# Moving a small projection from the first MLP to the end of layer 0's mixer, with one shared ring of scratch tiles

## The chip, the cores and the metric

The kernel runs on one core of a Trainium2 chip. The metric is the time of one execution on the device in microseconds (us), as the median of several runs; beside them stands one execution that was recorded by the hardware profiler, with a time of its own. Engines are named as the profile names them: PE is TensorE's matmuls and PEld its weight loads, DVE is VectorE, ACT is ScalarE, POOL is GpSimd, SP is SyncE, which here only issues the transfers of the weights.

## The reference, cut to what matters

A trunk of two layers works on x, 512 positions by 1024 features. Layer 0 mixes with a pair of recurrences (HGRN2 and RWKV-7), layer 1 with block attention. Each layer then has an MLP, and at its end a second input `p` (512 by 256 per layer) is projected, normalized and added through a gate:

```python
    for l in range(DEPTH):
        h = rms_norm(x, attn_norm[l])
        ...
        x = x + mix.astype(x.dtype)
        h = rms_norm(x, mlp_norm[l])
        x = x + jnp.square(jax.nn.relu(h @ w_up[l])) @ w_down[l]
        ple = rms_norm(p[l] @ ple_proj[l], ple_norm[l])
        x = x + ple * jax.nn.sigmoid(x @ ple_gate[l])
    return x
```

The line with `ple` depends on `p` and weights alone, not on x. It may be computed at any time before the gate of its layer.

## The kernel before, in words

**Tiles and products.** x lies transposed in SBUF as eight tiles of 128 features by 512 positions. Every large product is a `gemm` (line 240): a weight tile is stationary, 512 positions move, and each product is made of three matmuls, because weights and activations are split into a high and a low part (`mm3`, line 235). `wnext` (line 214) brings the weights: SyncE loads a half piece of 128 by 512 (line 223), ScalarE casts it to the high part `whi` (line 228), VectorE subtracts to get the low part `wlo` (line 229). The pieces come in a fixed order. While the mixer of layer 0 runs, there is one set of rings, two raw tiles and three of each part (`wa`, line 987). From the first MLP on a second set of three and four joins it (`wb`, line 992), so seven of each part.

**The order of the work.** The program is written as one long trace, and a planner turns it into a fixed order of instructions on each engine: it takes the instruction that was traced earliest among those whose inputs and buffers are ready by its estimate. So the text's order is a priority: what stands later fills gaps. `tc.high_priority` (line 720) puts the chain of the RWKV heads ahead of the rest. The work around the change comes in this order (`ORDER`, line 32, for four heads h):

- For each head: RWKV pieces (`step`, line 900, letters A and C), projections and HGRN recurrence (F, H), projections of the next head (B), and the output projection of the head before (O: `out_piece`, line 865). `hgrn` (line 731) takes its scratch from a ring of six tiles, `Hh` (line 364, `HB` in line 27), and its PSUM from `pmh`, a ring of two. Results of a head are split into tiles named `os`.
- `out_piece(3)` (line 928) stands alone behind the last head. Its eight evacuations add into x, then split and scale the new x for the MLP (`post`, line 979; lines 272 and 273) and square it (line 305), and GpSimd adds the squares up (`NormAcc`, line 311).
- The first MLP (`mlp`, line 1008). Its first four output tiles stay in PSUM (`pmr`, four tiles) until the row scale of the norm has been computed (`later_norm`, line 942): a chain of some ten tiny VectorE instructions on 128 by 4 values (lines 253 to 262, 292), then a broadcast over TensorE (`bcast_rows`, line 318, L326 in the profile).

**Delayed work.** `later` (line 933) holds functions with a count. `flush` (line 935) is called at each evacuation of the MLP's up projection and of the output projection, lowers each count and calls those that have run out. A count of 0 means the first call, 1 the second, and so on.

**The projection of the second input** is `ple` (line 949). It loads two tiles of `p` on ScalarE's queue (line 954), splits them into `act2` in layer 0 and `act` in layer 1, and multiplies two pieces of weights, each two half pieces giving four output tiles of 6 matmuls, through `pmh` (line 963): 48 matmuls. Each output tile is copied by ScalarE (line 959), squared by it, and GpSimd adds the squares. `finish` (line 966) computes the row scale, halves it (line 968), broadcasts it, and multiplies the eight tiles on VectorE (line 971). In layer 0 the projection itself is delayed (`PD` = 1, line 31): it is traced at the second evacuation of the first MLP, and `finish` four evacuations behind it (`FD` = 3, line 29). In layer 1 the projection is traced ahead of the attention's output projection (lines 1213 and 1214), and `finish` at the fourth evacuation of that. The eight output tiles are a pool of their own, `plp` (lines 1206 and 1212), until the gate (`gate`, line 1044) has read them.

**The values of the attention**, `vt` (line 1174), are one tile of 4 by 1024 per partition, written by ScalarE in eight pieces of 512 (line 1190) and read in slices of 128 columns (line 1167).

Of the kernel before, what the change touches and what calls it, by code (L numbers as in the profile page):

```python
# [11 lines left out]
F32 = mybir.dt.float32  # L12
F32R = mybir.dt.float32r
# [164 lines left out]
def trunk(ctx, tc, wts, xT, pT, vecs, lora, cst, lev, seg, rope, out, upto="all", dbg=None, mode=None):  # L178
# [97 lines left out]
    class Stats:  # L276
        def __init__(self, pool, tag, cols=1):
            self.n, self.cols, self.i = 1, cols, 0
            self.ps = pool.tile([P, 512], F32, name=tag)
# [16 lines left out]
            return (y, m) if both else y  # L296

    class NormAcc:
        def __init__(self, ring):
            self.ring, self.t = ring, None  # L300

        def add(self, src, eng="act"):
            sq = nrm.tile([P, S], F32, name="acc") if self.t is None else self.ring()
            if eng == "act":
                A.activation(sq, src, AF.Square)  # L305
            else:
                V.tensor_mul(sq, src, src)
            if self.t is None:
                self.t = sq
            else:  # L310
                G.tensor_add(self.t, self.t, sq)  # L311
# [39 lines left out]
    def chain(*gens):  # L351
        for g_ in gens:
            yield from g_


    def layer0_mixer(actp):
        ph = ExitStack()
# [3 lines left out]
        def E(name="e", bufs=EB, shape=None, dt=F32):  # L361
            return ex.tile(shape or [P, S], dt, name=name, bufs=bufs)

        def Hh():
            return ex.tile([P, S], F32, name="h", bufs=HB)

        BH = mp.tile([P, 2, 4, P], F32, name="BH")
        NAs = [mp.tile([P, 2, 2, 2, P], F32, name=f"NA{i}") for i in range(2)]
# [509 lines left out]

        lbo = VEC["lb"][0]
        e = [vec[:, lbo + 4 * i:lbo + 4 * i + 4] for i in range(3)]  # L880
        mx = mp.tile([P, 4], F32, name="lbm")
        V.tensor_max(mx, e[0], e[1])
        V.tensor_max(mx, mx, e[2])
        ee = mp.tile([P, 3, 4], F32, name="lbe")
        for i in range(3):
            V.tensor_sub(ee[:, i, :], e[i], mx)
        A.activation(ee, ee, AF.Exp)
        den = mp.tile([P, 4], F32, name="lbd")
        V.tensor_add(den, ee[:, 0, :], ee[:, 1, :])
        V.tensor_add(den, den, ee[:, 2, :])  # L890
        V.reciprocal(den, den)
        lb = mp.tile([P, 4], F32, name="lb")
        V.tensor_mul(lb, ee[:, 0, :], den)
        c1 = mp.tile([P, 4], F32, name="c1")
        V.tensor_scalar(c1, lb, 0.5, 0.5, op0=OP.mult, op1=OP.add)
        c2 = mp.tile([P, 4], F32, name="c2")
        V.tensor_scalar(c2, lb, -0.5, 0.5, op0=OP.mult, op1=OP.add)

        run(pre_h(0), p1(0, 0))
# [25 lines left out]
        for h in range(4):  # L925
            for c in ORDER:
                step(c, h)
        out_piece(3)
        ph.close()
        return acc, xg  # L930


    later = []

    def flush():
        for e in later[:]:
# [9 lines left out]
        later.append([n, lambda: nf.append(norm_rows(rt[0])[1])])  # L946
        return nf

    def ple(l, plp):
        pl = [plp.tile([P, S], F32, name=f"ple{m}") for m in range(8)]  # L950
        ps_ = []
        for k in range(2):
            t = tmp.tile([P, S], F32, name="r")
            nc.scalar.dma_start(t, pT[l, :, k, :])
            ps_.append(split(act if l else act2, t, "act" if l else "act2"))
        st = NormAcc(lambda: tmp.tile([P, S], F32, name="xsq"))

        def evac(m, ps):
            A.copy(pl[m], ps)
            st.add(pl[m])  # L960
        def body():
            for c in range(2):
                gemm(wnext(f"ple{l}", c), ps_, lambda m, ps: evac(4 * c + m, ps), nk=2, ring=pmh)
            later.append([FD[l], finish])

        def finish():
            rt = st.rs("n")
            V.tensor_scalar(rt, rt, 0.5, None, op0=OP.mult)
            rb = bcast_rows(rt, 1, pmh, "pmh")
            for m in range(8):  # L970
                V.scalar_tensor_tensor(pl[m], pl[m], vcol(f"pn{l}", m), rb, op0=OP.mult, op1=OP.mult)
        if l:
            body()
        else:
            later.append([PD, body])
        return pl

    act = ctx.enter_context(tc.tile_pool(name="act", bufs=16))
    def post(m, st, pool, tag, scale, dst):
# [6 lines left out]

    wa = wpool("wa", 2, 3)
    W["sets"] = [wa]
    st, xg = layer0_mixer(act)
    if upto == "mix0":  # L990
        return
    wb = wpool("wb", WB[0], WB[1])
# [71 lines left out]
    def attention(st, xg):  # L1064
# [72 lines left out]
        def head(h):  # L1137
            q, k, rq, nq = t.pop(h)
            pts = []
            for i in range(NJ):  # L1140
                n = (i + 1) * P
                ps = pmr.tile([P, S], F32, name="pmr")
                T.matmul(ps[:, :n], q[:, i * P:n], k[:, :n], start=True, stop=False)  # L1143
                T.matmul(ps[:, i * P:n], idb, cb, start=False, stop=True)
                mx = small.tile([P, 1], F32, name="mx")
                V.reduce_max(mx, ps[:, :n], axis=AX.X)
                V.tensor_mul(mx, mx, nq[:, i:i + 1])
                pt = ax.tile([P, n], F32, name=f"pt{i}")
                sm = small.tile([P, 1], F32, name="sm")
                A.activation(pt, ps[:, :n], AF.Exp, bias=mx, scale=rq[:, i:i + 1], accum_out=sm)  # L1150
                V.reciprocal(sm, sm)
                SCALE(pt, sm)
                pts.append(pt)
                yield
            pv = []
            for j in range(NJ):
                n = (NJ - j) * P
                ps = pmr.tile([P, S], F32, name="pmr")
                for i in range(j, NJ):
                    T.transpose(ps[:, (i - j) * P:(i - j + 1) * P], pts[i][:, j * P:j * P + P], ident)  # L1160
                tp = ax.tile([P, n], F32, name=f"pv{j}")
                A.copy(tp, ps[:, :n])
                pv.append(tp)
                yield
            ps = pmr.tile([P, S], F32, name="pmr")
            for j in range(NJ):
                T.matmul(ps[:, j * P:], vt[:, j, h * P:h * P + P], pv[j], start=j == 0, stop=j == NJ - 1)  # L1167
            res[h] = split(act2, ps, "act2")
            yield

        def SCALE(pt, sm):
            V.tensor_scalar(pt, pt, sm, None, op0=OP.mult)

        vt = ap.tile([P, NJ, D], F32, name="vt")

        def values(g, pools, after=None):
            ps = [p_.tile([P, S], F32, name=RING[p_]) for p_ in pools]
            for i in range(4):
                for z, (wh, wl) in enumerate(wnext("qkv", 4 * g + i)):
                    k = 2 * i + z  # L1180
                    for j in range(NJ):
                        xh, xl = (c[:, j * P:j * P + P] for c in xg[k])
                        T.matmul(ps[j], xh, wh, start=k == 0, stop=False)
                        T.matmul(ps[j], xh, wl, start=False, stop=False)
                        T.matmul(ps[j], xl, wh, start=False, stop=k == 7)
                if i == 1 and g == 0:
                    t["n"], m = st.rs("n", True)
                    V.tensor_scalar(e2, m, P * EPS, None, op0=OP.mult)
            for j in range(NJ):
                A.activation(vt[:, j, g * S:g * S + S], ps[j], AF.Copy, scale=t["n"][:, j:j + 1])  # L1190

        tc.keep_in_program_order(nc.scalar.preload_act_table_set("natural_log_exp_and_others"))
        values(0, [pmr] * 4)
# [9 lines left out]
        ph.close()  # L1203
        return [res[h] for h in range(8)]

    with tc.tile_pool(name="plp", bufs=1) as plp:
        nf = later_norm(st, ND[0])
        pl = ple(0, plp)
        xs = mlp(0, nf, xg)
        st, xg = gate(0, xs, pl)  # L1210
    o = attention(st, xg)
    with tc.tile_pool(name="plp", bufs=1) as plp:
        pl = ple(1, plp)
        st, xg = proj_out("o", o, 1)
        xs = mlp(1, later_norm(st, ND[1]), xg)
        gate(1, xs, pl)


OUT_SHAPE = (P, 8, S)
# [29 lines left out]
```

## Time and profile before

| | us |
|---|---|
| median of 3 runs (lowest to highest) | 1527.61 (1524.42 to 1528.14) |
| the profiled execution, its own time | 1525.94 |
| its span, from the first to the last instruction | 1524.2 |
| PE busy | 1487.4 (98%) |
| PEld busy | 1205.2 (79%) |
| DVE busy | 937.8 (62%) |
| ACT busy | 651.1 (43%) |
| POOL busy | 154.7 (10%) |

The mean granted clock of TensorE over the span is 0.997 of full. The span is about 1.7 us shorter than the execution's own time; that is the time around it. Times in the rows below count from the start of the span. Layer 0's mixer runs to about 465, the first MLP to about 820, its gate and the attention to about 1084, the attention's output projection to about 1128, and the second MLP and gate to the end.

A busy time of PE includes the pipeline: successive matmuls overlap, so the step from one start to the next is the time that one takes of the engine, and the length of one is longer. "[1.98 <-ACT os L269]" behind an instruction says that its engine had nothing to do for 1.98 us and that ScalarE's line 269, writing `os`, ended the wait.

### The profile page before, as it was taken

To read this page: it belongs to the slowest core of one execution; us is meant where nothing else is said; L and a number is where in the kernel's file an instruction comes from. 1 tells how busy PE (TensorE), PEld (TensorE's weight loads), DVE (VectorE), ACT (ScalarE), POOL (GpSimd) and SP (SyncE) were. 2 spreads that over 40 slices of the span, in tenths; PEclk is the share of its full clock that TensorE was granted. 3 is DMA by queue.
4 is the path that set the end of the run, shared out by engine and by line. 5 is a ranking of instruction groups with operands and counts; after the bars stand their busy time and mean duration, and the time that the engine had idled before them with its cause. 6 is when DMAs were issued, how large, how long until landed. Compare 5 with 4: busy or idle time off the path is not lost.

```text
span 1524.2 us, 20743 instructions
## 1 busy us (share of the span) xinstructions
PE 1487.4 (98%) x7656; PEld 1205.2 (79%) x7656; DVE 937.8 (62%) x1854; ACT 651.1 (43%) x1269; POOL 154.7 (10%) x145
## 2 busy tenths in 40 slices
PE   7999999999989999999999999999999999999998
PEld 5687787777667888888888888777778888888887
DVE  6877697686776644444446737777565444444463
ACT  3574544554446333333334533445634333333332
POOL 5221231211214000000000200000310000000000
PEclk9999999999999999999999999999999999999999
DMA  4211111201123333333333432111223333333331
GB/s 155 78 43 29 41 43 40 70 29 47 38 69 120 95 97 97 97 97 97 97 97 97 124 111 79 56 56 42 77 83 97 97 97 97 97 97 97 97 97 69
DMA packets 66966, 123.64 MB, mean 81 GB/s; under 512 B 7616, under 2 KB 8000, under 8 KB 66864
## 3 DMA queue, kind: packets, MB, share of 16 engines
q1 hardware_dynamic: 65376, 118.57, 25.6%
q10 hardware_dynamic: 1008, 2.16, 0.5%
q0 software_dynamic: 480, 1.57, 0.3%
q8 instruction: 60, 0.98, 0.3%
q14 instruction: 42, 0.34, 0.1%
HBM read 120.18 MB, written 2.10 MB: 80 GB/s over the span
## 4 chain that ended last, share of the span: by engine, by line
PE 90%; DVE 5%; ACT 2%; issue 1%; POOL 1%; DMA 1%; SPq 0%; DVEq 0%; POOLq 0%; ACTq 0%
PE pj L236 22%; PE pj L238 22%; PE pj L237 22%; PE pmr L237 2%; PE pmr L238 2%; PE pmr L236 2%; PE pmh L283 1%; PE pmr L1143 1%; PE pmr L1167 1%; PE pmr L596 1%; PE pmh L784 1%; DVE wlo L229 1%; DVE act L273 1%; PE pmr L532 1%; PE pmr L1160 1%
## 5 line engine op out<-in xcount | busy, mean ns | idle before, releaser
L228 ACT CAST whi<-wr 128x512 fp32r<-128x512 f32 x436 | 270.1, 621 | 605.2 <-PE pj L237 490.5
L229 DVE TENSOR_TENSOR wlo<-wr,whi 128x512 fp32r<-128x512 f32 x436 | 318.4, 733 | 215.5 <-ACT whi L228 195.9
L236 PE MATMUL pj<-act,whi 128*128 128x512 f32 (+1 forms) x968 | 384.3, 397 | 0.9 <-DVE h L858 0.9
L237 PE MATMUL pj<-act,whi 128*128 128x512 f32 (+1 forms) x968 | 381.9, 395 | 0.0
L238 PE MATMUL pj<-act,wlo 128*128 128x512 f32 (+1 forms) x968 | 381.4, 394 | 0.5 <-DVE wlo L229 0.5
L236 PEld LDWEIGHTS pj<-act,whi 128*128 128x128 f32 x968 | 182.6, 189 | 38.9 <-issue 2.3
L238 PEld LDWEIGHTS pj<-act,wlo 128*128 128x128 f32 x968 | 182.5, 189 | 36.9 <-DVE wlo L229 1.2
L237 PEld LDWEIGHTS pj<-act,whi 128*128 128x128 f32 x968 | 182.7, 189 | 35.0 <-issue 1.2
L238 PE MATMUL pj<-hid,wlo 128*128 128x512 f32 x512 | 199.4, 389 | 0.0
L237 PE MATMUL pj<-hid,whi 128*128 128x512 f32 x512 | 199.3, 389 | 0.0
L236 PE MATMUL pj<-hid,whi 128*128 128x512 f32 x512 | 199.3, 389 | 0.0
L1033 DVE TENSOR_TENSOR x<-x,pj 128x512 f32<-128x512 f32 x128 | 88.0, 688 | 80.7 <-PE pj L238 80.2
L236 PEld LDWEIGHTS pj<-hid,whi 128*128 128x128 f32 x512 | 96.1, 188 | 20.0
L238 PEld LDWEIGHTS pj<-hid,wlo 128*128 128x128 f32 x512 | 96.1, 188 | 20.0
L237 PEld LDWEIGHTS pj<-hid,whi 128*128 128x128 f32 x512 | 96.1, 188 | 19.9
L311 POOL TENSOR_TENSOR acc<-acc,xsq 128x512 f32<-128x512 f32 x28 | 38.6, 1379 | 627.3 <-ACT xsq L305 602.4
L1022 DVE SCALAR_TENSOR_TENSOR r<-pj,rb 128x512 f32<-128x512 f32 x56 | 38.7, 691 | 86.7 <-PE pj L238 86.7
L270 DVE TENSOR_TENSOR hid<-r,hid 128x512 fp32r<-128x512 f32 x64 | 44.3, 692 | 43.2 <-ACT hid L269 43.0
L236 PE MATMUL pmr<-act,whi 128*128 128x512 f32 x112 | 45.7, 412 | 6.7 <-ACT whi L228 6.7
L237 PE MATMUL pmr<-act,whi 128*128 128x512 f32 x112 | 45.7, 411 | 4.4 <-DVE act L273 4.4
L1023 ACT ACTIVATE r<-r 128x512 f32<-128x512 f32 x64 | 40.4, 632 | 20.9 <-DVE r L1022 20.9
L238 PE MATMUL pmr<-act,wlo 128*128 128x512 f32 x112 | 44.9, 405 | 0.0
(410 smaller groups left out, 2009.0 us busy)
## 6 DMA issues: line engine op xcount, KB each, us to landing
wr<-in_wts_dram SPq DMA_DIRECT2D x436, 256.0 KB, 2.7
x<-in_xT_dram SPq DMA_DIRECT2D x8, 256.0 KB, 6.5
out_dram<-x SPq DMA_DIRECT2D x7, 256.0 KB, 2.0
r<-in_pT_dram ACTq DMA_DIRECT2D x4, 256.0 KB, 3.7
lw<-in_lora_dram POOLq DMA_DIRECT2D x4, 192.0 KB, 3.1
tqn<-in_rope_dram ACTq DMA_DIRECT2D x1, 512.0 KB, 5.7
tkn<-in_rope_dram ACTq DMA_DIRECT2D x1, 512.0 KB, 6.2
cs<-in_cst_dram POOLq DMA_DIRECT2D x1, 289.0 KB, 5.8
```

What stands on the lines that cost most here:

```text
L228: A.copy(hi, raw)
L229: V.tensor_sub(lo, raw, hi.bitcast(F32))
L236: T.matmul(ps, wh, xh, start=first, stop=False)
L237: T.matmul(ps, wh, xl, start=False, stop=False)
L238: T.matmul(ps, wl, xh, start=False, stop=last)
L270: V.tensor_sub(l, src, h.bitcast(F32))
L273: V.scalar_tensor_tensor(l, src, scale, h.bitcast(F32), op0=OP.mult, op1=OP.subtract)
L283: T.matmul(self.ps[:, j * self.cols:(j + 1) * self.cols], sq[:, j * P:(j + 1) * P], rhs, start=(self.i == 0 and j == 0), stop=(self.i == s ...
L311: G.tensor_add(self.t, self.t, sq)
L1022: V.scalar_tensor_tensor(r, q, 0.0, nf[0], op0=OP.max, op1=OP.mult)
L1023: A.activation(r, r, AF.Square)
L1033: V.tensor_add(x[k], x[k], ps)
```

## The change

- In layer 0 the projection of the second input is traced at the end of the mixer, behind the last head's steps and ahead of `out_piece(3)`. It takes its working tiles from rings of the mixer that the last head no longer needs (`bo` and `y` for the loaded input, `r`, `k`, `v` and `kh` for its parts, `u` for the sum of squares, `e` for squares), and the weights through the mixer's one set of rings.
- `finish` is cut in two: `rows` computes and halves the row scale, `finish` broadcasts it and multiplies. In layer 0 `rows` is traced right behind `out_piece(3)` and `finish` at the second evacuation of the MLP. In layer 1 `rows` comes at the fourth evacuation of the output projection, where all of `finish` came before, and `finish` at the sixth.
- One ring `hp` of eight tiles named `h` takes the place of the mixer's ring of six, of the pool `plp`, and of `vt`: the mixer's scratch, the projection's eight results of each layer, and the eight tiles of the values take their turns in it.
- Four small tiles of the mixer are merged into two.

```diff
     class NormAcc:
-        def __init__(self, ring):
+        def __init__(self, ring, first=None):
             self.ring, self.t = ring, None
+            self.first = first or (lambda: nrm.tile([P, S], F32, name="acc"))
 
         def add(self, src, eng="act"):
-            sq = nrm.tile([P, S], F32, name="acc") if self.t is None else self.ring()
+            sq = self.first() if self.t is None else self.ring()
...
+    later = []
+    hp = None
+
+    def wide():
+        return hp.tile([P, S], F32, name="h")
+
...
-        def Hh():
-            return ex.tile([P, S], F32, name="h", bufs=HB)
+        Hh = wide
...
-        mx = mp.tile([P, 4], F32, name="lbm")
+        lbs = mp.tile([P, 2, 4], F32, name="lbs")
+        mx, den = lbs[:, 0, :], lbs[:, 1, :]
...
-        den = mp.tile([P, 4], F32, name="lbd")
...
-        c1 = mp.tile([P, 4], F32, name="c1")
+        cc12 = mp.tile([P, 2, 4], F32, name="c12")
+        c1, c2 = cc12[:, 0, :], cc12[:, 1, :]
         V.tensor_scalar(c1, lb, 0.5, 0.5, op0=OP.mult, op1=OP.add)
-        c2 = mp.tile([P, 4], F32, name="c2")
...
             for c in ORDER:
                 step(c, h)
+        pl, rows, finish = ple(0, lambda k: E("y" if k else "bo", 2),
+                               lambda i: E("r k v kh".split()[i], 1, dt=F32R),
+                               NormAcc(E, lambda: E("u", 1)))
         out_piece(3)
+        rows()
+        later.append([PD, finish])
         ph.close()
-        return acc, xg
-
-
-    later = []
+        return acc, xg, pl
+
...
-    def ple(l, plp):
-        pl = [plp.tile([P, S], F32, name=f"ple{m}") for m in range(8)]
+    def ple(l, raw, parts, st):
+
         ps_ = []
         for k in range(2):
-            t = tmp.tile([P, S], F32, name="r")
+            t = raw(k)
             nc.scalar.dma_start(t, pT[l, :, k, :])
-            ps_.append(split(act if l else act2, t, "act" if l else "act2"))
-        st = NormAcc(lambda: tmp.tile([P, S], F32, name="xsq"))
+            h, lo_ = parts(2 * k), parts(2 * k + 1)
+            A.copy(h, t)
+            V.tensor_sub(lo_, t, h.bitcast(F32))
+            ps_.append((h, lo_))
+        pl = []
 
         def evac(m, ps):
-            A.copy(pl[m], ps)
-            st.add(pl[m])
-        def body():
-            for c in range(2):
-                gemm(wnext(f"ple{l}", c), ps_, lambda m, ps: evac(4 * c + m, ps), nk=2, ring=pmh)
-            later.append([FD[l], finish])
+            t = wide()
+            A.copy(t, ps)
+            st.add(t)
+            pl.append(t)
+        for c in range(2):
+            gemm(wnext(f"ple{l}", c), ps_, evac, nk=2, ring=pmh)
+        rt = []
+
+        def rows():
+            r = st.rs("n")
+            V.tensor_scalar(r, r, 0.5, None, op0=OP.mult)
+            rt.append(r)
 
         def finish():
-            rt = st.rs("n")
-            V.tensor_scalar(rt, rt, 0.5, None, op0=OP.mult)
-            rb = bcast_rows(rt, 1, pmh, "pmh")
+            rb = bcast_rows(rt[0], 1, pmh, "pmh")
             for m in range(8):
                 V.scalar_tensor_tensor(pl[m], pl[m], vcol(f"pn{l}", m), rb, op0=OP.mult, op1=OP.mult)
-        if l:
-            body()
-        else:
-            later.append([PD, body])
-        return pl
+        return pl, rows, finish
...
     wa = wpool("wa", 2, 3)
     W["sets"] = [wa]
-    st, xg = layer0_mixer(act)
+    hp = ctx.enter_context(tc.tile_pool(name="hp", bufs=8))
+    st, xg, pl = layer0_mixer(act)
...
-                T.matmul(ps[:, j * P:], vt[:, j, h * P:h * P + P], pv[j], start=j == 0, stop=j == NJ - 1)
+                T.matmul(ps[:, j * P:], vt[j, h // 4][:, h % 4 * P:h % 4 * P + P], pv[j], start=j == 0, stop=j == NJ - 1)
...
-        vt = ap.tile([P, NJ, D], F32, name="vt")
+        vt = {}
...
-                A.activation(vt[:, j, g * S:g * S + S], ps[j], AF.Copy, scale=t["n"][:, j:j + 1])
+                vt[j, g] = wide()
+                A.activation(vt[j, g], ps[j], AF.Copy, scale=t["n"][:, j:j + 1])
...
-    with tc.tile_pool(name="plp", bufs=1) as plp:
-        nf = later_norm(st, ND[0])
-        pl = ple(0, plp)
-        xs = mlp(0, nf, xg)
-        st, xg = gate(0, xs, pl)
+    nf = later_norm(st, ND[0])
+    xs = mlp(0, nf, xg)
+    st, xg = gate(0, xs, pl)
     o = attention(st, xg)
-    with tc.tile_pool(name="plp", bufs=1) as plp:
-        pl = ple(1, plp)
-        st, xg = proj_out("o", o, 1)
-        xs = mlp(1, later_norm(st, ND[1]), xg)
-        gate(1, xs, pl)
+    pl, rows, finish = ple(1, lambda k: tmp.tile([P, S], F32, name="r"), lambda i: act.tile([P, S], F32R, name="act"),
+                           NormAcc(lambda: tmp.tile([P, S], F32, name="xsq")))
+    later.append([FD[1], rows])
+    later.append([FD[1] + 2, finish])
+    st, xg = proj_out("o", o, 1)
+    xs = mlp(1, later_norm(st, ND[1]), xg)
+    gate(1, xs, pl)
```

## Rows read from the trace of the kernel before

**Rows 1.** The page, busy time of each engine: us, share of span, instructions.

```profile
PE 1487.4 (98%) x7656; PEld 1205.2 (79%) x7656; DVE 937.8 (62%) x1854; ACT 651.1 (43%) x1269; POOL 154.7 (10%) x145
```

**Rows 2.** Windows: stretch, us, busy PE/PEld/DVE/ACT/POOL (instructions), granted clock, DMA share, GB/s.

```profile
60.00:395.00 335.00, 325.42 (x2337) 259.29 (x2337) 253.68 (x613) 176.77 (x408) 67.95 (x66) 1.00 0.15 43
440.00:466.00 26.00, 20.05 (x75) 14.50 (x75) 23.30 (x30) 16.05 (x29) 11.84 (x9) 0.93 0.33 98
455.30:458.70 3.40, 3.40 (x10) 2.60 (x9) 2.31 (x4) 2.38 (x4) 1.54 (x1) 0.51 0.53 143
472.00:486.00 14.00, 14.00 (x64) 11.57 (x63) 5.26 (x6) 11.59 (x22) 8.36 (x7) 1.00 0.28 85
1050.00:1104.60 54.60, 54.56 (x255) 41.83 (x255) 33.39 (x77) 33.92 (x74) 13.63 (x10) 1.00 0.21 64
1104.60:1111.00 6.40, 3.98 (x14) 3.12 (x13) 4.97 (x14) 0.62 (x1) 0.49 (x1) 0.73 0.16 41
```

**Rows 3.** Timeline of TensorE, layer 0: start us, us, instruction [idle before <-releaser].

```profile
442.44 0.50 PE L236 MATMUL pj<-os,whi 128*128 128x512 f32 x1 [1.98 <-ACT os L269]
...
446.77 0.51 PE L236 MATMUL pj<-os,whi 128*128 128x512 f32 x1 [0.78 <-DVE x L869]
...
454.52 0.74 PE L238 MATMUL pj<-os,wlo 128*128 128x512 f32 x2 [1.99 <-DVE wlo L229]
...
455.32 0.57 PE L238 MATMUL pmr<-act,wlo 128*128 128x512 f32 x1
...
458.68 0.45 PE L238 MATMUL pj<-os,wlo 128*128 128x512 f32 x1
...
488.66 0.60 PE L326 MATMUL pmh<-cs,rs_n 128*128 128x128 f32 x4
489.02 0.48 PE L236 MATMUL pmr<-act,whi 128*128 128x512 f32 x1
```

**Rows 4.** Tile pmh, 470 to 500 us: ns minimum/median/maximum, first and last start.

```profile
L236 PE MATMUL pmh<-act,whi x16: 388/389/392, 472.3 to 482.5; 128*128 128x512 f32 x16
```

**Rows 5.** Timeline of TensorE, layer 1.

```profile
1104.46 0.39 PE L238 MATMUL pj<-act,wlo 128*128 128x512 f32 x1
1107.27 1.09 PE L326 MATMUL pmh<-cs,rs_n 128*128 128x128 f32 x4 [2.42 <-DVE rs_n L968]
...
1110.96 0.39 PE L237 MATMUL pj<-act,whi 128*128 128x512 f32 x1
```

**Rows 6.** Timeline of VectorE, layer 1.

```profile
1099.95 0.16 DVE L292 TENSOR_SCALAR m_n<-pmh 128x4 f32<-128x4 f32 x1
...
1107.04 0.17 DVE L968 TENSOR_SCALAR rs_n<-rs_n 128x4 f32<-128x4 f32 x1
1108.39 5.36 DVE L971 SCALAR_TENSOR_TENSOR ple<-ple,vec,pmh 128x512 f32<-128x512 f32 x8 [1.18 <-PE pmh L326]
```

**Rows 7.** DMA issues, 440 to 470 us: count, KB each, us to landing.

```profile
wr<-in_wts_dram SPq DMA_DIRECT2D x12, 256.0 KB, 3.4
r<-in_pT_dram ACTq DMA_DIRECT2D x2, 256.0 KB, 3.8
```

**Rows 8.** TensorE's waits, 60 to 395 us: total us, times, longest.

```profile
PE pj L238 <- DVE wlo L229: 0.5, 2, 0.2
```

**Rows 9.** GpSimd's groups, 440 to 490 us: busy us, mean ns, idle before.

```profile
L311 POOL TENSOR_TENSOR acc<-acc,xsq 128x512 f32<-128x512 f32 x7 | 9.9, 1414 | 12.8 <-PE pmh L238 11.8 <-ACT xsq L305 0.7
```

**Rows 10.** VectorE's lines 229 and 869, 440 to 470 us.

```profile
L229 DVE TENSOR_TENSOR wlo<-wr,whi x12: 674/684/1793, 444.2 to 467.8; 128x512 fp32r<-128x512 f32 x12
...
L869 DVE TENSOR_TENSOR x<-x,pj x10: 675/680/689, 441.1 to 460.6; 128x512 f32<-128x512 f32 x10
```

**Rows 11.** Tile act, 464 to 472 us: the splitting of the second input.

```profile
L269 ACT CAST act<-r x2: 621/622/622, 468.5 to 469.2; 128x512 fp32r<-128x512 f32 x2
L270 DVE TENSOR_TENSOR act<-r,act x2: 685/689/693, 469.2 to 469.9; 128x512 fp32r<-128x512 f32 x2
```

**Rows 12.** Timeline of VectorE, layer 0: end of the MLP's row scale.

```profile
471.97 0.16 DVE L261 SCALAR_TENSOR_TENSOR rs_n<-ra_n,rs_n 128x4 f32<-128x4 f32 x1
```

## The prediction

> **What bounds the kernel now.** I read the page first: TensorE is busy for 1487.4 of the 1524.2 us span, the next engine for 62% [rows 1]. So only time in which TensorE stands still or runs at its lower clock can be won, and work that merely moves from one busy stretch to another is worth nothing. Next I cut the span into windows by stage, to see where TensorE is not full. The MLPs and the attention tail are full (14.00 of 14.00 us around the projection of layer 0, 54.56 of 54.60 us from the last heads to the middle of the output projection of layer 1) [rows 2]. Two stretches are not, and the change touches both: the end of layer 0's mixer (20.05 of 26.00 us) and a short hole in layer 1's output projection (3.98 of 6.40 us). Last I read TensorE's timeline in these two.
>
> In the first it waits 1.98 us at 442.44 for the split of the last heads' results, 0.78 us for an addition into x, 1.99 us for a weight's low part (line 229) [rows 3]; of the window's 5.95 idle us that leaves 1.2 in two small waits, 0.23 right behind the first and 0.98 for the last normalized tile. After the 1.99 us wait the granted clock falls: 0.51 from 455.3 to 458.7, the lower level of 1.2 GHz. Eight matmul steps there, from 455.32 to 458.68, last 3.36 us [rows 2, 3], where the same step takes 0.23 us at 2.4 GHz (the projection's own: 48 matmuls from 472.3 in 10.9 us [rows 4]), so 1.84 us; the clock costs 1.5 us. Lost from 440 to 466: 7.5 us.
>
> In the second, TensorE waits 2.42 us for `rs_n`, the row scale of layer 1's second-input projection [rows 5]. VectorE's timeline says why: the chain from its first small instruction at 1099.95 ends with L968 at 1107.04, some 7 us for some ten tiny instructions among large ones [rows 6], and the broadcast that needs it stands 5 us into that chain in TensorE's order. The mean clock over this window is 0.73 [rows 2]: matmuls after the broadcast go at the low level until 1110.71. From 1104.46 to 1110.96 pass 6.50 us. At the full clock it would be the matmul's 0.23, the broadcast's 0.36 (488.66 to 489.02 in layer 0 [rows 3]), 0.32 for the first matmul behind it (the next starts at 489.34) and six steps of 0.23: 2.29 us. Lost: 4.2 us.
>
> **The change, part by part.**
>
> *The projection of layer 0 moves* from the first MLP to before `out_piece(3)`. Its 48 matmuls (10.9 us) are the same in both places. Taken out of a full stretch, they shorten the MLP by 10.9 us; put in at 440, they lengthen the mixer's end by 10.9 us less what they cover. They are traced ahead of `out_piece(3)`, so they come first, and they need nothing of the chain that TensorE awaits at 442.44: the 1.98 and 0.23 us are covered whole. While they run VectorE does the work that had queued up behind that chain (the last additions of `out_piece(2)`, two splits, the first weights), so I take the 0.78 us as gone too. The 1.99 and 0.98 us come from VectorE falling behind `out_piece(3)` itself (23.30 us busy of 26.00 [rows 2]): the additions and normalized splits per tile are the same as before, so I leave these two, and the 1.5 us of clock. Gain: 1.98 + 0.23 + 0.78 = 2.99 us; bounds: 2.21 (the covered wait alone) and 7.5 (all of it).
>
> *What it adds there.* Weights now pass through the mixer's ring of three split tiles, where the MLP has seven. The projection adds four weight tiles to SyncE's queue in this place (256 KB, 3.4 us to landing [rows 7]), and three edges at which the second half of the next weight can only be split once the tile before is released: into its first piece, between its pieces, and out of it. The cost of an edge is not in the trace for this order. From below: 0, as in the MLP; from above 1.99 + 1.5 = 3.5 us, the one at 454.52 with its clock. Of the mixer's earlier edges only two left a wait on line 229, 0.5 us in all [rows 8]; I take 0.5 us each, near those: 1.5 us.
>
> *ScalarE and GpSimd.* Eight copies and eight squares move with the matmuls; in the MLP ScalarE was busy 11.59 of 14.00 us beside them [rows 2], and TensorE did not wait. Beside them now come the two splits of the last heads, 0.6 us each; I count nothing, covered by two PSUM tiles, and up to 1 us if that cover fails. GpSimd's seven additions into `acc` (1.41 us each [rows 9]) move as well, and here they meet VectorE's weight splits: line 229 takes 0.684 us at the median and 1.793 at the worst in this stretch, when GpSimd adds, while line 869, which has one operand in PSUM, stays between 0.675 and 0.689 us [rows 10]. The Trainium skill, "SBUF — State Buffer", section "SBUF: two separate sides", states that a VectorE instruction with two SBUF inputs and a GpSimd one lock each other out for a whole instruction; the trace agrees: 0.68 us plus one addition of 1.41 is an upper end that 1.79 does not pass. By the rule, with a block of 1.793 - 0.684 = 1.1 us at each of the three added edges, 3.3 us would stand in place of my 1.5, and the sum below would be 3.9 us. By the earlier edges few pay it, so I keep 1.5; the same contention, grown to a stall with the clock's fall, is the slower rival below.
>
> *The second input's loads.* Two 256 KB transfers on ScalarE's queue (3.8 us to landing [rows 7]), two casts and two subtractions (0.62 and 0.69 us [rows 11]) move to the last head, into tiles that are free once the head before is done. TensorE then has `out_piece(2)` to fill in; counted at nothing, and at most the 2.6 us of the two pairs of instructions if they delay the chain to 442.44, which the projection now covers.
>
> *Its scale* is finished at the second evacuation of the MLP: one broadcast and eight multiplications, 5.4 us of VectorE as in layer 1 [rows 6], where VectorE has 5.26 busy of 14.00 us today [rows 2]. The projection that left had stood ahead of the MLP's own broadcast at 488.66, whose scale was ready at 472.1 [rows 12]; without the 10.9 us that broadcast comes at about 477.8. Some 5.7 us of slack against a 5.4 us burst: counted at nothing, at worst a wait like layer 1's.
>
> *Layer 1.* `rows` runs where `finish` ran, the broadcast two evacuations later: two projection tiles of 24 matmuls, 2 x 5.45 us. The chain was 2.42 us late, so it is done 8 us early. The 5.4 us burst moves back by the same 11 us and stands ahead of two or three of the eight tiles' splits; TensorE has the first MLP tiles to fill in. Gain 4.2 us; bounds 2.4 (without the clock's part) and 4.2. That the first piece's tiles come free before the last heads end is worth nothing: TensorE has 0.04 us to win there [rows 2].
>
> *The ring of eight.* The mixer's scratch gets eight tiles for six, shared later with results and values; the values' evacuations are the same eight, into tiles whose readers are long past. In the heads TensorE is idle for 335.00 - 325.42 = 9.6 us in many small pieces [rows 2]. The planner will order them anew; from 3 us won to 3 us lost, a third of those pieces either way. I take 0.
>
> **Sum**: 2.99 - 1.5 + 4.2 = 5.7 us. The profiled execution took 1525.94 us, 1.67 below the median of 1527.61 of the runs shown; 1525.94 - 5.7 = 1520.2 on its own scale, 1521.9 against the median.
>
> **Rivals.**
> - *Layer 0 gives back what it covers.* The three edges cost 1 us each, or ScalarE's copies queue. For it: the ring of three and the full ScalarE. Against: the projection had no wait in the MLP. Only layer 1's gain stays: 1523.4.
> - *The wait moves into the first MLP.* The burst falls into the small instructions of the MLP's row scale, and the broadcast at 477.8 waits as layer 1's did. For it: slack and burst are alike in size. Against: the scale was ready before the burst can begin. 4.2 us come back: 1526.1.
> - *More is covered.* VectorE, relieved of the backlog at 442 to 446, keeps up with `out_piece(3)`, and the other waits and the clock's fall go as well: 7.5 + 4.2 = 11.7 less, 1515.9. Against: its work per tile is unchanged.
> - *The mixer's weight ring stalls* (slower). At each of the three edges line 229 is held up by GpSimd's moved additions, TensorE waits 2 to 3.5 us and the clock falls as at 455.3, so 3.5 to 5 us an edge, 12.8 in all at the middle: 12.8 - 2.99 - 4.2 = 5.6 more, 1533.2. It decides above 2.4 us an edge. Against: two of the mixer's earlier edges cost 0.5 us together.
> - *The order isn't what the text suggests*: the projection waits for PSUM or scratch of the last head and starts only at about 442. Then only layer 1 and the 0.78 us count, minus the edges: near the first rival, and counted with it.
>
> **How the numbers follow.** Forecast 0.42, more covered 0.15, layer 0 gives back 0.18, wait moves 0.13, ring stalls 0.12. About 0.3% (4.6 us, so 1523.0 and 1532.2) is what a measurement can tell from no change. The forecast's own spread is 1519 to 1524: 0.33 of its 0.42 fall below 1523.0. With 0.15, and 0.05 of the first rival, faster is 0.53; ring stalls gives slower 0.10; the rest, 0.37, is the same. The range leaves out most of the stalls and the best of the fourth case: 1515.5 to 1529.0.
>
> **What would show it.** In the changed profile: `pmh` matmuls right after 440 with no wait of 2 us for `os`; no wait of TensorE on `rs_n` in layer 1 and a granted clock of 1.00 in that window; TensorE full from the first MLP tile on; the waits on lines 229 and 273 around `out_piece(3)` still there. The forecast is wrong if waits of more than 1 us on line 229 or 228 stand at the projection's edges, if a broadcast waits in the first MLP, or if the idle time of 60 to 395 changes by more than 3 us.

## The result, and the profile after

The changed kernel is slower: 1559.46 us median (1557.04 to 1562.01, 4 runs) against 1527.32 us (1524.42 to 1528.14, 4 runs) for the kernel before, measured with it. The ratio is 1.0216, with a 95% interval of 1.0203 to 1.0229, so 33 us (31 to 35) where 5.7 us less were forecast. Both forecast mechanisms are there in the trace; what outweighs them is in two places that the sum put at nothing.

First the page of the changed kernel, busy time of each engine, to be laid beside [rows 1]:

```profile
PE 1500.1 (96%) x7656; PEld 1215.1 (78%) x7656; DVE 938.5 (60%) x1854; ACT 693.0 (44%) x1301; POOL 158.7 (10%) x145
```

The span is 1559.7 us, 35.5 longer, and PE's busy time grew by 12.7 only: two thirds of the loss is TensorE standing still. One other number stands out. ScalarE issues 1301 instructions where it issued 1269, and is busy 41.9 us longer, although the change gives it no work. Dividing, the 32 new instructions take 1.3 us each.

The next step is to cut the span by stage. The windows of the changed kernel (stretch, us, busy PE, PEld, DVE, ACT, POOL with instructions, granted clock, DMA share, GB/s):

```profile
440.00:466.00 26.00, 23.65 (x105) 17.57 (x104) 20.07 (x40) 15.87 (x30) 12.81 (x9) 1.00 0.36 111
...
500.00:820.00 320.00, 320.00 (x1414) 264.95 (x1413) 162.33 (x245) 114.21 (x184) 0.00 (x0) 1.00 0.32 97
...
820.00:920.00 100.00, 100.00 (x447) 82.92 (x446) 55.62 (x88) 46.44 (x76) 9.02 (x7) 1.00 0.37 114
920.00:1080.00 160.00, 140.68 (x690) 107.61 (x688) 97.95 (x256) 94.78 (x178) 0.00 (x0) 0.99 0.18 53
1080.00:1120.00 40.00, 36.05 (x153) 25.68 (x154) 19.65 (x62) 26.50 (x62) 7.00 (x6) 0.87 0.07 21
1120.00:1160.00 40.00, 40.00 (x184) 33.23 (x183) 30.70 (x50) 18.60 (x31) 9.89 (x8) 1.00 0.29 88
```

The end of layer 0's mixer is fuller than it was (23.65 of 26 us; it was 20.05 [rows 2]), the first MLP is full, and layer 1's output projection, which now falls into 1120 to 1160, is full at a clock of 1.00. The hole is new: 19.3 idle us between 920 and 1080, in the heads of the attention, a stretch that the change hardly touches, and it goes on behind 1080 at a lower clock. In the kernel before the same stretch reads:

```profile
920.00:1080.00 160.00, 159.96 (x802) 122.84 (x801) 111.72 (x310) 73.26 (x193) 1.92 (x2) 1.00 0.17 52
```

TensorE's waits in the changed kernel from 920 to 1125 (total us, times, longest) have three names:

```profile
PE pmh L327 <- DVE rkn L1126: 12.4, 6, 2.8
PE pmr L1180 <- ACT pv L1175: 9.3, 6, 2.6
PE pmh L283 <- ACT sq L1103: 1.3, 2, 0.7
```

`rkn` is the row scale of a head's keys, computed by a logarithm (L1122) and an exponential (L1123) on ScalarE, and `pv` a part of its softmax, behind L1163. ScalarE's groups of the changed kernel (instructions, busy us, mean ns of one) show what came ahead of these:

```profile
L1122 ACT ACT_TABLE_LOAD x16 | 20.5, 1283 | 0.3
L1123 ACT ACT_TABLE_LOAD x14 | 18.0, 1283 | 0.2
...
L1163 ACT ACT_TABLE_LOAD x2 | 2.6, 1283 | 0.0
```

Here are the 32 instructions: loads of an activation table, 1283 ns each, one ahead of the logarithm and one ahead of the exponential of nearly every row scale. The kernel before has none in its attention. It loads one set that holds both functions, once, by a preload (line 1192) that `tc.keep_in_program_order` pins behind the ScalarE instruction traced ahead of it, which is the load of the causal mask `cf` (line 1073). ScalarE's timeline of the kernel before, around the last Tanh of gate 0:

```profile
866.82 0.59 ACT L1049 ACTIVATE r<-pj 128x512 f32<-128x512 f32 x1
868.27 0.33 ACTq L1070 DMA_DIRECT2D tqn<-in_rope_dram  x1
869.01 0.34 ACTq L1070 DMA_DIRECT2D tkn<-in_rope_dram  x1
869.38 0.85 ACTq L1073 DMA_DIRECT2D cf<-in_cst_dram  x1
870.27 1.28 ACT L1192 ACT_TABLE_LOAD   x1
```

And of the changed kernel, around the first Tanh of gate 0:

```profile
833.74 0.33 ACTq L1086 DMA_DIRECT2D cf<-in_cst_dram  x1
834.37 1.28 ACT L1206 ACT_TABLE_LOAD   x1
835.66 1.28 ACT L1062 ACT_TABLE_LOAD   x1
836.96 0.60 ACT L1062 ACTIVATE r<-pj 128x512 f32<-128x512 f32 x1
```

By the order in which the program opens and closes its pools, the attention's pool `ap` lay over `plp`, the pool of the projection's results, which gate 0 reads to its end; so the mask's load was placed behind the last Tanh (a run below moves the mask alone). The change does away with `plp`. The load now goes ahead of the first Tanh, the preload follows it, and the Tanh loads its own set over it 1.29 us later. From then on the preloaded set is gone, and each function brings its own. A single row scale shows the price, in ScalarE's timeline of the changed kernel:

```profile
961.95 1.28 ACT L1122 ACT_TABLE_LOAD   x1
963.24 0.21 ACT L1122 ACTIVATE akn<-vkn 128x4 f32<-128x4 f32 x1
963.35 0.60 ACT L228 CAST whi<-wr 128x512 fp32r<-128x512 f32 x1
963.97 1.28 ACT L1123 ACT_TABLE_LOAD   x1
965.27 0.20 ACT L1123 ACTIVATE rkn<-akn 128x4 f32<-128x4 f32 x1
```

and TensorE's broadcast of this scale, in its timeline, waits 2.76 us, little more than the two loads (2.57 us):

```profile
966.83 0.79 PE L327 MATMUL pmh<-cs,rkn 128*128 128x128 f32 x4 [2.76 <-DVE rkn L1126]
```

The Trainium skill, "ScalarE: Activation LUTs", section "What ACT_TABLE_LOAD costs", gives 1283 ns for the load and a drain of some 1380 ns with each switch. The load agrees to the nanosecond. The drain doesn't show here: the cast ends at 963.95, the load begins at 963.97, and the exponential starts 1.30 us after that. The measurement decides; a switch costs this kernel 1.3 us of ScalarE.

The second place is the mixer. TensorE's waits in the changed kernel from 60 to 440:

```profile
PE pmh L770 <- DVE h L765: 5.8, 3, 2.7
...
PE pmr L470 <- DMA lw<-in_lora_dram: 2.0, 1, 2.0
```

In the kernel before the first is, from 60 to 400,

```profile
PE pmh L764 <- DVE h L759: 1.0, 2, 0.6
```

and 0.3 from there to 500, and the second 0.5. The last head's copy of values (`A.copy(vt, ...)`) starts at 400.3 where it started at 395.2: 5.1 us are gone by then. TensorE's idle time from 60 to 395 is 335.00 - 321.84 = 13.2 us; it was 9.6.

### The profile page after: what moved, and what is told of

It reads as the page before. It is cut to its first block, busy times and chain, and to the rows that moved or that the text cites. A ratio compares the mean times of both kernels' runs of the same rounds, so it can differ in the third digit from the quotient of the medians.

```text
span 1559.7 us, 20768 instructions
## 1 busy us (share of the span) xinstructions
PE 1500.1 (96%) x7656; PEld 1215.1 (78%) x7656; DVE 938.5 (60%) x1854; ACT 693.0 (44%) x1301; POOL 158.7 (10%) x145
## 4 chain that ended last, share of the span: by engine, by line
PE 85%; ACT 6%; DVE 5%; issue 2%; DMA 1%; POOL 0%; SPq 0%; ACTq 0%; DVEq 0%; POOLq 0%
PE pj L236 21%; PE pj L237 21%; PE pj L238 20%; PE pmr L237 1%; PE pmh L790 1%; PE pmr L238 1%; PE pmr L236 1%; PE pmh L283 1%; ACT L1122 1%; PE pmr L1180 1%; PE pmr L1156 1%; PE pmr L602 1%; ACT L1123 1%; DVE wlo L229 1%; PE pmr L538 1%
## 5 line engine op out<-in xcount | busy, mean ns | idle before, releaser
L312 POOL TENSOR_TENSOR acc<-acc,xsq 128x512 f32<-128x512 f32 x21 | 29.4, 1401 | 650.3 <-ACT xsq L306 632.2
```

## The experiments

Four theories are kept apart by the runs. T: the attention's table loads cost some 31 us, because the preload slipped ahead of gate 0. R: the ring of eight `h` tiles costs the mixer some us. S: splitting layer 1's finish gains some 4 us. F: the projection at the mixer's end gains some 1.5 us, as forecast. Every kernel here computes the whole reference. The kernel before measured 1526.8 us (1524.45 to 1528.43, 21 runs) beside the runs of the preload (in both kernels), of the ring of eight and of the split; 1526.7 us beside those of the mask and of the ring of six; and 1526.9 us beside that of the move. Ratios are to it, and a time saved or lost against it is worked out from the ratio, which need not be the difference of the two medians.

**The preload ahead of the attention's loads**, in the changed kernel; the rest stays as it is:

```diff
         ax = ph.enter_context(tc.tile_pool(name="ax", bufs=2))
+        tc.keep_in_program_order(nc.scalar.preload_act_table_set("natural_log_exp_and_others"))
...
-        tc.keep_in_program_order(nc.scalar.preload_act_table_set("natural_log_exp_and_others"))
         values(0, [pmr] * 4)
```

> The changed kernel, with the preload of the Ln and Exp table set traced at the head of the attention instead of behind its three loads. Theory T (tables): the changed kernel loads 32 more table sets of 1.28 us because the preload, pinned behind the load of the causal mask, slipped ahead of the first gate's Tanh; put back behind the gate, the 16 + 14 + 2 loads in the attention go and with them 30 to 35 us: 1524 to 1530 us, 10 table loads in all. Rival V (values): the attention is slower because the values' eight tiles share one ring with the projection and the scratch; then the time stays at 1555 to 1560 us.

1528.59 us (1523.62 to 1532.2, 12 runs), ratio 1.0012 (1.0001 to 1.0023): by the medians 30.9 us less than the changed kernel. The preload now lands at 880.0, behind gate 0, and ScalarE is back at 1269 instructions, with 11 table loads, as many as the kernel before has (10 were expected). The window that had the hole:

```profile
920.00:1080.00 160.00, 160.00 (x806) 123.48 (x805) 114.48 (x315) 73.60 (x191) 3.00 (x3) 1.00 0.19 59
```

**The same fault put into the kernel before**: its preload is traced ahead of gate 0.

```diff
     xs = mlp(0, nf, xg)
+    tc.keep_in_program_order(nc.scalar.preload_act_table_set("natural_log_exp_and_others"))
     st, xg = gate(0, xs, pl)
```

(and the one in the attention goes)

> The kernel before, with nothing changed but the place of that preload: traced between the first MLP and the gate of layer 0. Theory T: Tanh loads its set again, 30 table loads or more appear in the attention, and the time rises by 30 to 35 us, to 1557 to 1563 us. Rival V: the values are still one tile, so the time stays at 1527 us, give or take 3.

1556.15 us (1553.67 to 1560.37, 4 runs), ratio 1.0201 (1.0184 to 1.0217), just under the range that theory T gave, and far from V's; TensorE's first wait between 900 and 1110 is the same as in the changed kernel:

```profile
PE pmh L326 <- DVE rkn L1113: 12.4, 6, 2.7
```

So the preload's place alone is worth about 31 us in either kernel (here 28 to 33). What set that place is still open here.

**The mask in another pool**, in the kernel before:

```diff
-        cf = ap.tile([P, P], F32, name="cf")
+        cf = const.tile([P, P], F32, name="cf")
```

> The kernel before with one word changed: the causal mask's tile is taken from the pool of constants, not from attention's pool, so its load needn't wait until the space of the results' pool is free. Nothing is computed otherwise and no pool of the first MLP changes. Theory T with its cause (the pinned table preload follows the instruction traced ahead of it, the mask's load, and that load's time was set by when the space under it came free): the mask's load and the preload leave their place behind gate 0, the mixer's and gate's ScalarE functions load their own set again, and attention's Ln and Exp then load a table each time: about 31 more table loads of 1.28 us each, most of them in attention, and 1553 to 1562 us, as in e2_before_preload_early. Rival P (it is the number of buffers or the order of the first MLP, not the space under the mask, that let the preload slip in the changed kernel): 1526 to 1529, with 11 table loads as before.

1560.13 us (1557.75 to 1562.29, 4 runs), ratio 1.0225 (1.021 to 1.0241). One word costs 2%. Outside `ap` the mask's load needs to wait for nothing, and ScalarE's timeline shows it, and the preload behind it, at the very start of the kernel:

```profile
0.74 0.41 ACTq L1073 DMA_DIRECT2D cf<-in_cst_dram  x1
...
2.70 1.28 ACT L1192 ACT_TABLE_LOAD   x1
```

The two other loads of the attention, which stay in `ap`, keep their place behind the last Tanh (872.84 and 873.58 us, the Tanh at 871.38). The preloaded set was thrown out by the mixer's first functions long before the attention, which pays as the changed kernel does (`rkn` 12.4 us again). The last head of the mixer also starts 4.5 us late here (its copy of values at 399.7), with the ring of six; why is open. The place of the preload was an accident of which memory lay under a 64 KB tile.

**The ring of eight alone**, in the kernel before, with the small tiles merged as in the change to make room:

```diff
-HB = 6
+HB = 8
```

> The kernel before, with nothing but the mixer's ring of eight scratch tiles for six (and the four small tiles merged into two so that it fits). Theory R (ring): with more tiles GpSimd runs three subtractions of a level ahead in a row, VectorE's two-operand products beside them take 1.3 to 1.6 us for 0.7, TensorE waits for L765 in the heads and its clock falls: the heads end 5 us later, 1531 to 1534 us. Rival M (moved work): the delay in the heads comes from the second input's loads and casts that moved into the last head, so the ring alone gives 1526 to 1529 us.

1534.54 us (1531.72 to 1538.24, 6 runs), ratio 1.0057 (1.0042 to 1.0071): 8.7 us (6.4 to 10.8) slower, half a us above the range that theory R gave, with the copy of the last head's values at 401.9. TensorE's waits from 60 to 440 have the changed kernel's line again:

```profile
PE pmh L764 <- DVE h L759: 5.7, 3, 2.7
```

What a bigger ring does to it is seen in GpSimd's groups, 60 to 440, of the kernel before (busy us, mean ns, idle before and what ended it):

```profile
L776 POOL TENSOR_TENSOR h<-h 128x512 f32<-128x512 f32 x20 | 24.3, 1230 | 21.5 <-DVE KS L780 14.5 <-PE pmh L736 6.1 <-PE pmh L764 0.8
```

and of this run:

```profile
L776 POOL TENSOR_TENSOR h<-h 128x512 f32<-128x512 f32 x20 | 24.7, 1253 | 12.6 <-DVE KS L780 6.8 <-PE pmh L736 4.3 <-PE pmh L764 1.4
```

GpSimd's twenty subtractions, one for each level of the recurrence, used to wait 14.5 us for VectorE to be done with an older tile; with two more tiles they wait 6.8 and run early. There they meet VectorE's product of line 759, which TensorE awaits: in the last head of the kernel before (tile `h`, ns minimum, median, maximum, first and last start) it is

```profile
L759 DVE TENSOR_TENSOR h<-h x1: 679/679/679, 402.1 to 402.1; 128x512 f32<-128x512 f32 x1
```

and in this run

```profile
L776 POOL TENSOR_TENSOR h<-h x5: 1108/1487/1537, 406.7 to 413.0; 128x512 f32<-128x512 f32 x5
...
L759 DVE TENSOR_TENSOR h<-h x1: 1579/1579/1579, 408.7 to 408.7; 128x512 f32<-128x512 f32 x1
```

The Trainium skill, "SBUF — State Buffer", section "SBUF: two separate sides", has a VectorE instruction with two SBUF inputs and a GpSimd one that reads SBUF shut each other out for a whole instruction. The rows agree as far as they go: 1.58 us is the 0.68 of the product and 0.90 more, which is less than one subtraction of 1.49. Behind the longer waits the clock falls: TensorE waits 2.69 us for L759 at 192.24 and 1.86 us at 299.55, and the mean granted clock is 0.66 from 190 to 200 and 0.83 from 300 to 310, where the kernel before has 1.00 in both. So the 8.7 us are waits and clock together.

**The ring of six again, in the changed kernel.** With the preload ahead, and the seventh and eighth result and value tile under a name of their own, which the mixer doesn't use:

```diff
-    def wide():
-        return hp.tile([P, S], F32, name="h")
+    def wide(i=0):
+        return hp.tile([P, S], F32, name="h", bufs=6) if i < 6 else hp.tile([P, S], F32, name="g", bufs=2)
...
-            t = wide()
+            t = wide(len(pl))
...
-                vt[j, g] = wide()
+                vt[j, g] = wide(4 * g + j)
```

> The changed kernel with the preload ahead (as in e1_preload_first), and the ring of eight divided by name: the mixer has its six h tiles again, and two tiles of another name take the seventh and eighth result and value tile. So the projection still lies at the mixer's end and layer 1's finish is still split, but the mixer can no longer run further ahead than before. Theory R (with eight h tiles GpSimd's subtractions come out early beside VectorE's two-input products and cost 5 to 8 us over the mixer's heads): the time goes from 1528.6 down to 1520.5 to 1523.5; the wait pmh L770 <- DVE h L765 is back near 1.2 us in 60 to 400 us and the copies of the heads are back within 1 us of before's times. Rival M (it is the projection's place at the mixer's end that slows layer 0, and the ring only did so beside it): 1526 to 1529, with the heads on before's times but the last x add of the first MLP still over 17 us late. Against e4_before_split_finish (1522.6), which has the split alone: lower by 1 to 2 us if the covered waits of the old place are worth what the difference of e1, e3 and e4 gives (1.7), the same or higher if the move is worth nothing.

1521.66 us (1520.12 to 1523.66, 8 runs), ratio 0.9969 (0.9959 to 0.9979). It needs no more memory than the changed kernel, and it is faster than the kernel before. The wait is back at

```profile
PE pmh L770 <- DVE h L765: 1.0, 2, 0.6
```

from 60 to 400, GpSimd waits 14.5 us for `KS` as it used to, and the copy of values starts at 395.2. That undoing the ring brings back the wait, the durations and the 7 us together is what the runs show; that the lock between the two engines carries it from one to the other is read from the rows, and no run separates it from the mere change of order.

**The split of layer 1's finish alone**, in the kernel before:

```diff
-            later.append([FD[l], finish])
+            if l:
+                later.append([FD[l], rows])
+                later.append([FD[l] + 2, finish])
```

(cut; `rows` and `finish` are two functions as in the change, and layer 0 keeps both at one place)

> The kernel before, with nothing but layer 1's finish cut in two (scale at the fourth evacuation of the output projection, broadcast and products at the sixth). Theory S: the wait of 2.4 us on the row scale and the clock's fall behind it go, nothing comes in their place: 4.2 us less, 1522 to 1524.5 us. Rival: the products' 5.4 us of VectorE delay the last tiles and TensorE waits at the front of the second MLP instead: 1526 to 1529 us.

1522.6 us (1521.06 to 1524.39, 9 runs), ratio 0.9976 (0.9966 to 0.9985): 3.7 us (2.3 to 5.2) less. The broadcast has no wait, and the stretch that lost 4.2 us is full and at the upper level (timeline of TensorE, then the window):

```profile
1111.31 0.60 PE L326 MATMUL pmh<-cs,rs_n 128*128 128x128 f32 x4
```

```profile
1104.00:1111.00 7.00, 7.00 (x32) 5.79 (x32) 6.22 (x16) 2.38 (x4) 2.80 (x3) 1.00 0.26 74
```

**The move of layer 0's projection alone**: the kernel with the ring of six, and layer 1's finish in one piece again.

```diff
-    later.append([FD[1], rows])
-    later.append([FD[1] + 2, finish])
+    later.append([FD[1], lambda: (rows(), finish())])
```

> As e5_six_plus_two, but layer 1's row sums and finish are again one piece at the old place, so that against the kernel before only the move of layer 0's projection to the mixer's end is left (with the mixer's ring of six, and the preload where it does no harm). Theory F (the forecast's term: 2.99 us of waits covered, less about 1.5 of weight waits): 1524.5 to 1525.9, under the kernel before by 1 us or more. Theory Z (the covered waits come back as waits inside the projection itself: in e5_six_plus_two its second weight tile is waited for 2.24 us and its second chunk 0.44 us, in place of 1.98 and 0.78 us, and the clock falls to its lower level for some us after): within 1 us of the kernel before, 1525.9 to 1527.7. Theory W (the move costs, as the profiles of e4 and e5 have it: gate 0 first 829.3 and 830.7 us): 1527.7 to 1529. In all three the wait for the row scale in layer 1 (2.42 us in the kernel before) is back.

1524.44 us (1522.28 to 1527.77, 11 runs), ratio 0.9989 (0.998 to 0.9998): 1.7 us (0.3 to 3.1) less, nearest to theory F's 1.5; the interval also holds the upper part of Z's (a gain under 1 us), and Z's waits are there. TensorE's timeline of this run shows them:

```profile
445.88 0.98 PE L238 MATMUL pmh<-v,wlo 128*128 128x512 f32 x2 [2.25 <-DVE wlo L229]
447.11 0.80 PE L236 MATMUL pmh<-r,whi 128*128 128x512 f32 x1 [0.25 <-ACT h L972]
```

Nothing waits for `os` any more; in its place the projection's second weight tile is awaited for 2.25 us, and the mean granted clock from 440 to 450 is 0.83. VectorE's timeline of this run says why:

```profile
443.33 0.69 DVE L270 TENSOR_TENSOR os<-h,os 128x512 fp32r<-128x512 f32 x1 [0.63 <-ACT os L269]
443.94 0.68 DVE L875 TENSOR_TENSOR x<-x,pj 128x512 f32<-128x512 f32 x1
444.53 0.69 DVE L270 TENSOR_TENSOR os<-e,os 128x512 fp32r<-128x512 f32 x1
445.14 3.09 DVE L229 TENSOR_TENSOR wlo<-wr,whi 128x512 fp32r<-128x512 f32 x5
```

In VectorE's order the projection's weights stand behind the splits of `os`, the very chain that the projection was to cover, so TensorE waits for that chain by way of the weights. GpSimd is idle from 442.7 to 448.7, so it is not its contention that holds the weights up here. The 1.99 us wait on line 229 inside the old `out_piece(3)` shrank in turn, to 1.0 us in two waits, and the 0.78 us for x is gone. Layer 1's wait for `rs_n` is back, 2.4 us.

## Why the prediction was wrong

**The step that failed** is in the part on the ring of eight: "the values' evacuations are the same eight, into tiles whose readers are long past", counted at nothing. It asked who still reads the new place, and not what the old place had been holding back. `plp` was named as a pool that the change removes, its eight tiles held "until the gate", and no step priced what had waited for that memory: the attention's two tables, its mask, and the preload pinned behind them. The parts counted the loads that the change moves in its text, not those that it sets free. 30.9 us hang on that.

**The ring in the mixer** had the right place and the wrong size. The forecast let the small pieces of 60 to 395 go "from 3 us won to 3 us lost", and took 0; alone it costs 8.7 us (6.4 to 10.8), outside both ends. Its bound was a third of TensorE's idle time there, as if only existing gaps could move. What grew was the duration of a VectorE instruction that TensorE awaits, 0.68 to 1.58 us. The rows read like the contention with GpSimd that the prediction saw in [rows 10] and looked for only at the weights, though no run parts it from the change of order; and behind the waits the clock fell. One of the prediction's own signs of being wrong came true here: the idle time of 60 to 395 rose by 3.6 us, more than the 3 us it allowed.

**The covered waits of layer 0**: 2.99 less 1.5, so 1.5 us; 1.7 (0.3 to 3.1) in the run of the move alone. The sum held, its parts did not, so that it held is in part luck. In that run the waits for `os` were not covered but came back at the projection's first edge, 2.25 us where 0.5 was taken and with the clock's fall behind it; against that, 1.0 of the 1.99 us that the forecast left in place was gained, and the other edges cost little. In the changed kernel itself, with the heads in another order, TensorE waits 1.6 us at 440 to 500 for ScalarE's copy (L972), which was priced at up to 1 us if its cover failed.

**Layer 1**: 4.2 us forecast, 3.7 (2.3 to 5.2) measured by the split alone; the kernels with and without it at a ring of six differ by 0.9989 - 0.9969, or 3.1 us. Right.

**The first MLP** was put at nothing and is full: 320.00 us of 320.00 in the windows above. Right, so the rival with the burst in the MLP is out. The slower rival, a stall of the weight ring, gave 1533.2 by another mechanism; the longest wait on line 229 from 440 to 500 in the changed kernel is 1.2 us, so that stall is not there. That the kernel came out slower is no point for it.

The terms measured one by one add up, as far as their intervals tell: 30.9 + 8.7 - 1.7 - 3.7 = 34.2 us, against 33 (31 to 35) for the whole. Without the first two terms the change is what was forecast: 4.7 us (3.2 to 6.3) less in the version with the ring of six and the preload ahead, against 5.7.

## What to carry to other kernels

When a change removes or moves a buffer, list what used to wait for its memory, and above all which loads and preloads were pinned behind those; a start that is right only because a tile underneath was late should be pinned to what it really must follow. A larger ring is no free gift: it can let one engine's work run early into another engine's critical instruction. In a profile, compare instruction counts before times: 32 more instructions on an engine without new work named the cause in one line.

## What the runs showed of the hardware that was not expected

The same order and the same waits in one head left TensorE at different clocks. In the changed kernel it waits 1.19 us for L765 at 408.80 and 0.39 us at 410.35, and then runs at the lower of its two levels (1.2 GHz); with the ring of eight in the kernel before it waits 1.17 and 0.39 us in the same two places, and stays at 2.4 GHz. The windows, first of the changed kernel:

```profile
415.00:420.00 5.00, 5.00 (x23) 4.62 (x23) 3.20 (x10) 0.72 (x2) 0.93 (x1) 0.50 0.01 3
```

then of the ring of eight in the kernel before:

```profile
415.00:420.00 5.00, 4.42 (x35) 3.66 (x34) 4.26 (x12) 1.68 (x4) 1.71 (x2) 1.00 0.01 3
```

These are two profiled executions, 1.5 us apart in that head, and the second has small waits of its own instead. The 1.5 us are not what parts them: the changed kernel with the preload ahead has the same two waits within 0.04 us of the second's times (1.17 us before 410.29, 0.39 before 411.85), and goes down to 0.50 from 415 to 420 as well. Nor need the program differ: the ring of six and the move alone run the same matmuls in the same order here, and from 476 to 486 the first has a mean clock of 0.83, the second 1.00, behind waits of 0.94 and 1.20 us for L273. What decided between them no run here shows. The fall at 415 is not what the ring costs: the last head was already 5.1 and 6.7 us late ahead of it (its copy of values at 400.3 and 401.9, for 395.2), and the run that kept its clock there still broadcasts the MLP's row scale at 494.83, 6.2 us behind the 488.66 of [rows 3].
